# Side loads on GpSimd's queue, and the column sum of each pair's left halves by an accumulating load

## The chip, the cores and the metric

The kernel runs on one core of one Trainium2 chip. The core has TensorE (matrix products), VectorE, ScalarE (ACT here), GpSimd (POOL) and SyncE (SP), which run side by side and wait for one another by semaphores; 16 DMA engines move data between HBM and SBUF. A DMA is issued by an instruction on the queue of SP, ACT or GpSimd. The metric is the device time of one execution in microseconds. A profiled execution also leaves a trace, from which the rows below are.

## The reference, cut to what matters

One layer of a decoder trunk on 256 tokens of width 2048, all in float32: an input norm; one projection `w_in` to three mixers and their gates; the mixers (a gated short convolution, a causal spatial gating, a 31-tap convolution branch), each projected by `w_branch`, gated and summed; an output projection and a norm; a feed-forward net and a norm.

```
x = layer_norm(x, ln_in_g, ln_in_b)
z = x @ w_in                                   # 2048 -> 13312
merged = sum over n of sigmoid(g_n + gate_bias_n) * (y_n @ w_branch[n])
mix = merged @ w_out                           # 2048 -> 2048
x = layer_norm(2**0.25 * x + mix, ln_mix_g, ln_mix_b)
h_gate, h_up = split(x @ w_ffn_in)             # 2048 -> 2 x 5632
ffn = (silu(h_gate) * h_up) @ w_ffn_out        # 5632 -> 2048
x = layer_norm(2**0.25 * x + ffn, ln_ffn_g, ln_ffn_b)
```

The kernel reads some 300 MB of weights once, and multiplies each by the 256 tokens, held as two blocks of 128.

## The kernel before, in words

**Split products.** TensorE works in float32r. A float32 operand is split in two float32r parts: `hi` is the cast (ACT, L128), `lo` is what the cast left off (VectorE, L130). A product is three matrix products: hi·hi, hi·lo, lo·hi (L205 to L207 in `gemm`, L251 to L253 in `product`). Every weight tile goes through this split, which is by far the largest work of ACT and VectorE.

**The plan.** `plan` is one list of 552 weight tiles of 512 KB, in the order of use. A tile of a plain chunk is two blocks of 128 rows by 512 columns; a tile of a block product (`add_block`) is 128 rows by 1024 columns, a left and a right half. `pump(i)` is called before each step of a product: it loads up to 5 tiles ahead (`load_one`, L184, on SP's queue, four buffers `wraw`), splits up to 3 ahead (`split_one`; seven buffers each of `whi` and `wlo`), and runs up to two pieces of background work. The program order of loads and splits follows from that; in time they run as far ahead as the buffers let them.

**Pairs.** In a block product, some pairs of weight rows are done by a scheme of seven products instead of eight (Strassen's, in Winograd's form): 57 pairs, two or three to a block. A pair takes two tiles, `t0` and `t1`, whose halves are called b12, b11 (left and right of `t0`) and b22, b21 (of `t1`). `split_pair` (L133 to L161) makes on VectorE the sums t1 = b11+b12, t3 = b12+b22 (in place, over b12), t2 = t1+b22 and t4 = t2+b21, in the tile `tsum` and in `wraw`, four additions of 128 x 512 (L140), and splits four tiles: `second` (`t1`), `low` (t1 and t2), `first` (`t0`, now t3 and b11) and `last` (t4). `gemm_block` then takes them in the order second, low, first, last: products with b21, b22, t1, t2, b11, t3, t4. A step of a single tile is 12 matrix products of 512 columns, a pair 21. After a block's last pair one ACT copy (L295) and four VectorE additions (L296 to L299) combine the shared sums; the block's four results are evacuated after its last step (`evac`, with `total`, L656). A block of the branches, of `ac`, `ah`, `ab` and of `o` has six singles, a pair, three singles, a pair, three singles; the feed-forward blocks have three pairs (gate blocks `fg` and up blocks `fu`, numbered by the first of their two column groups f) or two (`fo`). A switch ADDER, off, would have made two of the additions by accumulating DMAs from SBUF.

**The order around the change.** `clock` counts steps (a pair is two). `defer(fn, after)` puts work off by so many steps; `run_deferred` runs what is due after each step. Each engine takes its instructions in the program's order, so an instruction that waits holds up what stands behind it on its engine. Scratch rows of 128 x 512 come from a pool of 8, `tmp`.

**The output projection `o`.** The block ("o", 0) makes column groups 0 and 1 (clock 0 to 16), two plain chunks of 8 steps groups 2 and 3. Their results are added to the normed input, scaled: `residual(j)` (L811 to L819) broadcasts 512 entries of `ln_in_g` and `ln_in_b` to all partitions (two DMAs on ACT's queue, L804), loads the two token blocks of x into `R` (SP, L815), and does two VectorE operations on each (L816, L818). It was due at clock 7, 9, 11 and 13 for j = 0 to 3. `R` lies in a pool opened (`open_ffn`) in place of those of the branches, so its first writer waits for their last readers, the transposes of `merged`. `evac_o` (L823, L825) adds the projection and takes norm statistics.

**Feed-forward.** Eleven column groups in three parts. `mix_residual(j)` (two broadcasts by L804, then L849 and L850 on `R`) is run in the up blocks f = 0 and f = 2. The last norm's eight rows are loaded by the same `bcast` (L804) before the last two chunks. Norm statistics end with two small GpSimd operations (L325, L328).

Of the kernel before, what the change touches and what calls it, by code (L numbers as in the profile page):

```python
# [41 lines left out]
SUMS_AT = 5  # L42
X_PAIRS = 2
LEAD = 6
ADDER = False

OFF_AB, OFF_AC, OFF_AH = 0, DA, 2 * DA
OFF_BU, OFF_BV = 3 * DA, 4 * DA
# [5 lines left out]
def trunk_kernel(ctx: ExitStack, tc: tile.TileContext, x, ln_in_g, ln_in_b, w_in, gate_bias,  # L54
# [23 lines left out]
    def cols(j, w=NW):  # L78
        return slice(j * w, (j + 1) * w)
# [53 lines left out]
    def split_pair(t0, t1):  # L133


        b12, b11, b22, b21 = t0[:, 0, :], t0[:, 1, :], t1[:, 0, :], t1[:, 1, :]
        ts = wp.tile([P, 3, NW], F32, name="tsum", bufs=1)

        def add(out, a, b):
            nc.vector.tensor_tensor(out=out, in0=a, in1=b, op=ALU.add)  # L140

        add(ts[:, 0, :], b11, b12)
        if ADDER:
            nc.gpsimd.dma_start(out=b12, in_=b22, accum_op=ALU.add)
        else:
            add(b12, b12, b22)
        add(ts[:, 1, :], ts[:, 0, :], b22)
        second = split_tile(t1)
        if ADDER:
            nc.scalar.copy(out=ts[:, 2, :], in_=ts[:, 1, :])  # L150
            nc.gpsimd.dma_start(out=ts[:, 2, :], in_=b21, accum_op=ALU.add)
        else:
            add(ts[:, 2, :], ts[:, 1, :], b21)
        low = split_tile(ts[:, 0:2, :])
        first = split_tile(t0)
        last = split_tile(ts[:, 2:3, :], 1)

        def part(pair, i):
            return pair[0][:, i, :], pair[1][:, i, :]

        return {"b11": part(first, 1), "t3": part(first, 0), "b22": part(second, 0), "b21": part(second, 1),  # L161
                "t1": part(low, 0), "t2": part(low, 1), "t4": part(last, 0)}
# [18 lines left out]
    def load_one():  # L181
        j = state["dma"]
        t = wp.tile([P, KT, NW], F32, name="wraw", bufs=RAW_BUFS)
        nc.sync.dma_start(out=t, in_=plan[j])  # L184
        raw_t[j] = t
        state["dma"] += 1

    def may_split():
# [23 lines left out]
    def defer(fn, after=DEFER, banks=True):  # L212


        deferred.append((clock[0] + after, fn, banks))
# [585 lines left out]

    def bcast(src, j):
        t_ = new_tmp()
        nc.scalar.dma_start(out=t_, in_=src[0:1, cols(j)].broadcast_to([P, NW]))  # L804
        return t_

    stm = stats_tile("stm", 4)
    lg2, lb2 = (a.rearrange("(o d) -> o d", o=1) for a in (ln_in_g, ln_in_b))
    res = {}

    def residual(j):  # L811
        gj, bj = bcast(lg2, j), bcast(lb2, j)
        for t in range(NT):
            xr = res[t, j] = R[t][:, cols(j)]
            nc.sync.dma_start(out=xr, in_=x2d[cols(t, P), cols(j)])  # L815
            nc.vector.scalar_tensor_tensor(out=xr, in0=xr, scalar=mv_in[t][:, 0:1], in1=gj,  # L816
                                           op0=ALU.subtract, op1=ALU.mult)
            nc.vector.scalar_tensor_tensor(out=xr, in0=xr, scalar=rs_in[t], in1=bj,  # L818
                                           op0=ALU.mult, op1=ALU.add)  # L819

    def evac_o(t, j, ps, add=None):
        dst = R[t][:, cols(j)]
# [13 lines left out]
            for q in range((S_PAIRS + 1) // 2):  # L836
                defer(lambda q=q: token_sums(xS, 2 * q, kept[0, q], kept[1, q], min(2, S_PAIRS - 2 * q)), 6 + q, False)

    for j in range(4):
        defer(lambda j=j: residual(j), 7 + 2 * j, False)  # L840
    gemm_block(("o", 0), mT, lambda i, t, h, ps, add: evac_o(t, h, ps, add), mTS)
    for j in (2, 3):
        gemm(("o", j), mT, lambda t, ps, j=j: evac_o(t, j, ps), skew=SKEW if j == 3 else 0)

    def mix_residual(j):
        gj, bj = bcast(ln_mix_g, j), bcast(ln_mix_b, j)
        for t in range(NT):
            cs = R[t][:, cols(j)]
            nc.vector.scalar_tensor_tensor(out=cs, in0=cs, scalar=ALPHA, in1=gj, op0=ALU.mult, op1=ALU.mult)  # L849
            nc.vector.scalar_tensor_tensor(out=cs, in0=bj, scalar=ALPHA, in1=cs, op0=ALU.mult, op1=ALU.add)  # L850


    stf = stats_tile("stf", 4)
# [99 lines left out]
```

## Time and profile before

| | us |
|---|---|
| Median of 3 runs (lowest to highest) | 1556.21 (1555.82 to 1557.3) |
| The profiled execution, device time | 1555.2 |
| Its span in the trace | 1553.5 |
| TensorE busy | 1522.1 |
| VectorE busy | 1340.1 |
| ACT busy | 771.1 |
| GpSimd busy | 16.4 |

The span is from the first to the last instruction that the profile shows; the 1.7 us around it belong to the device time. Busy times count an engine's work once, however much of it overlaps; register and semaphore instructions and the issue of DMAs are not in them. In rows, PE is TensorE's products, PEld its weight loads, DVE VectorE; a `q` after an engine's name means its sequencer, which issues DMAs. `out<-in` names the tiles, L the line. PEclk is the granted clock as a share of full speed. An engine's idle time in brackets stands before the instruction, with what ended it.

### The profile page before, as it was taken

Reading aid. Unit: us, or ns where it says so; the run is one execution under the profiler, and the core shown is the slowest. Engines: PE = TensorE matmul, PEld = TensorE weight load, DVE = VectorE, ACT = ScalarE, POOL = GpSimd, SP = SyncE. Lnnn points to the kernel's source line nnn. Section 1 sums busy time; section 2 is a strip of 40 time slices with the busy share of each in tenths; the row PEclk is TensorE's granted clock in tenths of the full one; section 3 lists DMA queues with packets and bytes.
Section 4 is the critical chain, followed back from the end, with each engine's and each line's share of the span. In section 5 each row is a group of like instructions: output and inputs, shape, how many; then the busy total and the mean of one; then the engine's idle time right before and its main releaser. Section 6 shows DMA issues by size and latency. Waiting matters only on the chain. (4 is left out here: it accounts for less than half of the span.)

```text
span 1553.5 us, 18790 instructions
## 1 busy us (share of the span) xinstructions
PE 1522.1 (98%) x6799; PEld 1247.2 (80%) x6799; DVE 1340.1 (86%) x1792; ACT 771.1 (50%) x885; POOL 16.4 (1%) x28
## 2 busy tenths in 40 slices
PE   7999999999999999999999999999999999999997
PEld 5888888888888888888877888788888878888885
DVE  7699999987789878778879799988899988889677
ACT  5544445444455454545426454555555554455451
POOL 1000000000000000000000000000000000000000
PEclk9999999999999999999999999999999999999999
DMA  6866656566665665756755666566665666666654
GB/s 215 277 191 186 182 150 227 167 220 199 201 204 161 217 201 182 251 169 228 239 181 162 218 190 215 178 229 204 191 195 171 202 193 199 205 190 203 217 176 149
DMA packets 105363, 308.13 MB, mean 198 GB/s; under 512 B 9908, under 2 KB 11028, under 8 KB 105270
## 3 DMA queue, kind: packets, MB, share of 16 engines
q1 hardware_dynamic: 99158, 295.38, 60.2%
q10 hardware_dynamic: 6112, 11.55, 2.5%
q8 instruction: 53, 0.87, 0.2%
q14 instruction: 40, 0.33, 0.1%
HBM read 304.80 MB, written 2.10 MB: 198 GB/s over the span
## 5 line engine op out<-in xcount | busy, mean ns | idle before, releaser
L128 ACT CAST whi<-wraw 128x1024 fp32r<-128x1024 f32 x551 | 577.2, 1051 | 539.3 <-PE acc L253 152.3
L130 DVE TENSOR_TENSOR wlo<-wraw,whi 128x1024 fp32r<-128x1024 f32 x551 | 666.4, 1220 | 127.7 <-ACT whi L128 124.1
L251 PE MATMUL acc<-whi,th 128*128 128x512 f32 x1235 | 485.7, 393 | 2.1 <-ACT th L316 1.0
L252 PE MATMUL acc<-wlo,th 128*128 128x512 f32 x1235 | 481.6, 390 | 0.0
L253 PE MATMUL acc<-whi,tl 128*128 128x512 f32 x1235 | 481.1, 390 | 0.0
L251 PEld LDWEIGHTS acc<-whi,th 128*128 128x128 f32 x1235 | 231.9, 188 | 52.0 <-ACT th L316 1.8
L253 PEld LDWEIGHTS acc<-whi,tl 128*128 128x128 f32 x1235 | 231.7, 188 | 50.3 <-DVE tl L317 0.3
L252 PEld LDWEIGHTS acc<-wlo,th 128*128 128x128 f32 x1235 | 232.0, 188 | 47.5
L206 PE MATMUL acc<-wlo,th 128*128 128x512 f32 x496 | 194.6, 393 | 3.4 <-DVE wlo L130 3.4
L205 PE MATMUL acc<-whi,th 128*128 128x512 f32 x496 | 195.7, 395 | 0.2 <-ACT th L316 0.2
L207 PE MATMUL acc<-whi,tl 128*128 128x512 f32 x496 | 194.4, 393 | 0.0
L128 ACT CAST whi<-tsum 128x1024 fp32r<-128x1024 f32 x114 | 95.3, 836 | 145.6 <-DVE tsum L140 122.6
L130 DVE TENSOR_TENSOR wlo<-tsum,whi 128x1024 fp32r<-128x1024 f32 x114 | 108.5, 952 | 12.5 <-ACT whi L128 12.5
L206 PEld LDWEIGHTS acc<-wlo,th 128*128 128x128 f32 x496 | 93.8, 189 | 23.5 <-DVE wlo L130 4.1
L207 PEld LDWEIGHTS acc<-whi,tl 128*128 128x128 f32 x496 | 93.8, 189 | 20.2 <-DVE tl L317 0.4
L205 PEld LDWEIGHTS acc<-whi,th 128*128 128x128 f32 x496 | 93.7, 189 | 20.1 <-ACT th L316 0.8
L563 DVE SCALAR_TENSOR_TENSOR cv<-pad,cw,cv 128x256 f32<-128x256 f32 x240 | 101.4, 482 | 0.0
L140 DVE TENSOR_TENSOR tsum<-tsum,wraw 128x512 f32<-128x512 f32 x114 | 78.1, 685 | 0.6
L251 PE MATMUL acc<-whi,yh 128*128 128x512 f32 x192 | 75.7, 394 | 0.0
L252 PE MATMUL acc<-wlo,yh 128*128 128x512 f32 x192 | 75.5, 393 | 0.0
L253 PE MATMUL acc<-whi,yl 128*128 128x512 f32 x192 | 74.7, 389 | 0.0
L140 DVE TENSOR_TENSOR tsum<-wraw 128x512 f32<-128x512 f32 x57 | 39.2, 688 | 29.9 <-DMA wraw<-in_w_in_dram 21.1
(157 smaller groups left out, 1172.0 us busy)
## 6 DMA issues: line engine op xcount, KB each, us to landing
wraw<-in_w_in_dram SPq DMA_DIRECT2D x208, 512.0 KB, 4.0
wraw<-in_w_ffn_in_dram SPq DMA_DIRECT2D x176, 512.0 KB, 4.3
wraw<-in_w_ffn_out_dram SPq DMA_DIRECT2D x88, 512.0 KB, 4.5
wraw<-in_w_branch_dram SPq DMA_DIRECT2D x48, 512.0 KB, 5.0
wraw<-in_w_out_dram SPq DMA_DIRECT2D x32, 512.0 KB, 6.2
gb<-in_gate_bias_dram ACTq DMA_DIRECT2D x12, 256.0 KB, 3.4
R<-in_x_dram SPq DMA_DIRECT2D x8, 256.0 KB, 4.6
x<-in_x_dram SPq DMA_DIRECT2D x2, 512.0 KB
```

The costliest lines, as they stand in the source:

```text
L128: nc.scalar.copy(out=hi, in_=t)
L130: nc.vector.tensor_tensor(out=lo, in0=t, in1=hi.bitcast(F32), op=ALU.subtract)
L140: nc.vector.tensor_tensor(out=out, in0=a, in1=b, op=ALU.add)
L205: nc.tensor.matmul(ps, lhsT=xh[:, k, ts], rhs=hi[:, kk, :], start=first, stop=False)
L206: nc.tensor.matmul(ps, lhsT=xh[:, k, ts], rhs=lo[:, kk, :], start=False, stop=False)
L207: nc.tensor.matmul(ps, lhsT=xl[:, k, ts], rhs=hi[:, kk, :], start=False, stop=last)
L251: nc.tensor.matmul(ps, lhsT=ah, rhs=bh, start=first, stop=False)
L252: nc.tensor.matmul(ps, lhsT=ah, rhs=bl, start=False, stop=False)
L253: nc.tensor.matmul(ps, lhsT=al, rhs=bh, start=False, stop=last)
L563: nc.vector.scalar_tensor_tensor(out=cv[:, b, :], in0=pad[:, b, q:q + S], scalar=w_, in1=cv[:, b, :], op0=ALU.mult, op1=ALU.add)
```

## The change

`load_one` issues, right behind the load of a pair's first tile, a second DMA on GpSimd's queue, which reads the left half of the second tile (b22) from HBM and adds it to the left half of the first (b12) where that lies in SBUF. So t3 = b12+b22 needs no VectorE addition. `split_pair` splits the second tile first, and then makes three additions, from it: t2 = b11 + t3, t1 = t2 - b22, t4 = t2 + b21; `first` is split before `low`. The switch ADDER goes.

The row broadcasts of `bcast` are issued on GpSimd's queue instead of ACT's. The eight x loads of the residual are issued together on GpSimd's queue at clock 3 (`residual_rows`) instead of on SP's. `residual(j)` issues its broadcasts at clock 5, 7, 15 and 17 and its VectorE operations four steps later, at 9, 11, 19 and 21; `mix_residual` keeps its place, with its VectorE operations three steps after its broadcasts.

```diff
--- before.py
+++ after.py
@@ -42,7 +42,6 @@
 SUMS_AT = 5
 X_PAIRS = 2
 LEAD = 6
-ADDER = False
 
 OFF_AB, OFF_AC, OFF_AH = 0, DA, 2 * DA
 OFF_BU, OFF_BV = 3 * DA, 4 * DA
@@ -136,23 +135,15 @@
         b12, b11, b22, b21 = t0[:, 0, :], t0[:, 1, :], t1[:, 0, :], t1[:, 1, :]
         ts = wp.tile([P, 3, NW], F32, name="tsum", bufs=1)
 
-        def add(out, a, b):
-            nc.vector.tensor_tensor(out=out, in0=a, in1=b, op=ALU.add)
-
-        add(ts[:, 0, :], b11, b12)
-        if ADDER:
-            nc.gpsimd.dma_start(out=b12, in_=b22, accum_op=ALU.add)
-        else:
-            add(b12, b12, b22)
-        add(ts[:, 1, :], ts[:, 0, :], b22)
+        def add(out, a, b, op=ALU.add):
+            nc.vector.tensor_tensor(out=out, in0=a, in1=b, op=op)
+
         second = split_tile(t1)
-        if ADDER:
-            nc.scalar.copy(out=ts[:, 2, :], in_=ts[:, 1, :])
-            nc.gpsimd.dma_start(out=ts[:, 2, :], in_=b21, accum_op=ALU.add)
-        else:
-            add(ts[:, 2, :], ts[:, 1, :], b21)
+        add(ts[:, 1, :], b11, b12)
+        add(ts[:, 0, :], ts[:, 1, :], b22, ALU.subtract)
+        add(ts[:, 2, :], ts[:, 1, :], b21)
+        first = split_tile(t0)
         low = split_tile(ts[:, 0:2, :])
-        first = split_tile(t0)
         last = split_tile(ts[:, 2:3, :], 1)
 
         def part(pair, i):
@@ -183,6 +174,8 @@
         t = wp.tile([P, KT, NW], F32, name="wraw", bufs=RAW_BUFS)
         nc.sync.dma_start(out=t, in_=plan[j])
         raw_t[j] = t
+        if j in fast:
+            nc.gpsimd.dma_start(out=t[:, 0, :], in_=plan[j + 1][:, 0, :], accum_op=ALU.add)
         state["dma"] += 1
 
     def may_split():
@@ -801,22 +794,27 @@
 
     def bcast(src, j):
         t_ = new_tmp()
-        nc.scalar.dma_start(out=t_, in_=src[0:1, cols(j)].broadcast_to([P, NW]))
+        nc.gpsimd.dma_start(out=t_, in_=src[0:1, cols(j)].broadcast_to([P, NW]))
         return t_
 
     stm = stats_tile("stm", 4)
     lg2, lb2 = (a.rearrange("(o d) -> o d", o=1) for a in (ln_in_g, ln_in_b))
-    res = {}
-
-    def residual(j):
+    def residual_rows():
+        for j in range(4):
+            for t in range(NT):
+                nc.gpsimd.dma_start(out=R[t][:, cols(j)], in_=x2d[cols(t, P), cols(j)])
+
+    def residual(j, wait):
         gj, bj = bcast(lg2, j), bcast(lb2, j)
-        for t in range(NT):
-            xr = res[t, j] = R[t][:, cols(j)]
-            nc.sync.dma_start(out=xr, in_=x2d[cols(t, P), cols(j)])
-            nc.vector.scalar_tensor_tensor(out=xr, in0=xr, scalar=mv_in[t][:, 0:1], in1=gj,
-                                           op0=ALU.subtract, op1=ALU.mult)
-            nc.vector.scalar_tensor_tensor(out=xr, in0=xr, scalar=rs_in[t], in1=bj,
-                                           op0=ALU.mult, op1=ALU.add)
+
+        def go():
+            for t in range(NT):
+                xr = R[t][:, cols(j)]
+                nc.vector.scalar_tensor_tensor(out=xr, in0=xr, scalar=mv_in[t][:, 0:1], in1=gj,
+                                               op0=ALU.subtract, op1=ALU.mult)
+                nc.vector.scalar_tensor_tensor(out=xr, in0=xr, scalar=rs_in[t], in1=bj,
+                                               op0=ALU.mult, op1=ALU.add)
+        defer(go, wait, False)
 
     def evac_o(t, j, ps, add=None):
         dst = R[t][:, cols(j)]
@@ -836,18 +834,22 @@
             for q in range((S_PAIRS + 1) // 2):
                 defer(lambda q=q: token_sums(xS, 2 * q, kept[0, q], kept[1, q], min(2, S_PAIRS - 2 * q)), 6 + q, False)
 
-    for j in range(4):
-        defer(lambda j=j: residual(j), 7 + 2 * j, False)
+    defer(residual_rows, 3, False)
+    for j, at in enumerate((5, 7, 15, 17)):
+        defer(lambda j=j: residual(j, 4), at, False)
     gemm_block(("o", 0), mT, lambda i, t, h, ps, add: evac_o(t, h, ps, add), mTS)
     for j in (2, 3):
         gemm(("o", j), mT, lambda t, ps, j=j: evac_o(t, j, ps), skew=SKEW if j == 3 else 0)
 
     def mix_residual(j):
         gj, bj = bcast(ln_mix_g, j), bcast(ln_mix_b, j)
-        for t in range(NT):
-            cs = R[t][:, cols(j)]
-            nc.vector.scalar_tensor_tensor(out=cs, in0=cs, scalar=ALPHA, in1=gj, op0=ALU.mult, op1=ALU.mult)
-            nc.vector.scalar_tensor_tensor(out=cs, in0=bj, scalar=ALPHA, in1=cs, op0=ALU.mult, op1=ALU.add)
+
+        def go():
+            for t in range(NT):
+                cs = R[t][:, cols(j)]
+                nc.vector.scalar_tensor_tensor(out=cs, in0=cs, scalar=ALPHA, in1=gj, op0=ALU.mult, op1=ALU.mult)
+                nc.vector.scalar_tensor_tensor(out=cs, in0=bj, scalar=ALPHA, in1=cs, op0=ALU.mult, op1=ALU.add)
+        defer(go, 3, False)
 
 
     stf = stats_tile("stf", 4)
```

## Rows read from the trace of the kernel before

**Rows 1.** The page's first part: busy us, share of the span, instructions

```profile
PE 1522.1 (98%) x6799; PEld 1247.2 (80%) x6799; DVE 1340.1 (86%) x1792; ACT 771.1 (50%) x885; POOL 16.4 (1%) x28
```

**Rows 2.** Stretches: us, busy PE, PEld, DVE, ACT, POOL; PEclk; DMA share; GB/s

```profile
0.00:40.00 40.00, 29.42 (x127) 20.41 (x128) 31.67 (x52) 23.18 (x41) 5.93 (x12) 0.91 0.68 217
...
760.00:800.00 40.00, 36.55 (x154) 29.73 (x153) 31.83 (x40) 14.31 (x15) 0.00 (x0) 0.96 0.53 175
...
960.00:1000.00 40.00, 38.71 (x167) 30.89 (x167) 37.63 (x47) 17.95 (x21) 0.00 (x0) 1.00 0.63 189
...
1080.00:1120.00 40.00, 40.00 (x177) 32.87 (x176) 37.31 (x45) 20.26 (x22) 0.00 (x0) 1.00 0.64 195
...
1240.00:1280.00 40.00, 37.56 (x169) 29.49 (x168) 35.78 (x45) 19.76 (x23) 0.00 (x0) 1.00 0.63 191
...
1520.00:1560.00 40.00, 22.43 (x99) 18.22 (x98) 23.63 (x33) 3.16 (x3) 3.41 (x4) 0.90 0.33 120
```

**Rows 3.** TensorE's waits: for whom, us in total, times, longest

```profile
PE acc L310 <- DVE tmp L432: 9.3, 6, 3.4
PE acc L206 <- DVE wlo L130: 3.4, 1, 3.4
...
PE acc L252 <- DVE wlo L130: 1.2, 2, 0.8
```

**Rows 4.** A group of instructions on VectorE: busy us, mean ns, idle before, releasers

```profile
L140 DVE TENSOR_TENSOR wraw<-wraw 128x512 f32<-128x512 f32 x57 | 39.2, 687 | 17.7 <-DMA wraw<-in_w_in_dram 11.7 <-DMA wraw<-in_w_ffn_out_dram 3.5 <-DMA wraw<-in_w_ffn_in_dram 2.0
```

**Rows 5.** Timeline of VectorE, 774 to 787: start us, us, instruction

```profile
776.59 1.42 DVE L816 SCALAR_TENSOR_TENSOR R<-R,mvin,tmp 128x512 f32<-128x512 f32 x2 [1.80 <-DMA tmp<-in_ln_in_g_dram]
779.46 1.41 DVE L818 SCALAR_TENSOR_TENSOR R<-R,rsin,tmp 128x512 f32<-128x512 f32 x2 [1.46 <-DMA tmp<-in_ln_in_b_dram]
...
786.77 1.22 DVE L130 TENSOR_TENSOR wlo<-wraw,whi 128x1024 fp32r<-128x1024 f32 x1
```

**Rows 6.** Stretches of 10 us around the `o` block's evacuation

```profile
790.00:800.00 10.00, 10.00 (x39) 8.07 (x39) 6.00 (x6) 4.34 (x5) 0.00 (x0) 0.86 0.77 255
800.00:810.00 10.00, 10.00 (x46) 8.27 (x45) 6.95 (x8) 3.03 (x3) 0.00 (x0) 1.00 0.80 269
```

**Rows 7.** L184 from 978 to 979.5, and VectorE's timeline from 986

```profile
L184 SPq DMA_DIRECT2D wraw<-in_w_ffn_in_dram x1: 327/327/327, 978.7 to 978.7; - x1
...
DMA to landing us min/median/max: 4.4/4.4/4.4
...
988.06 1.22 DVE L130 TENSOR_TENSOR wlo<-wraw,whi 128x1024 fp32r<-128x1024 f32 x1
```

**Rows 8.** Timelines of VectorE and TensorE, third pairs of f=4 and f=6

```profile
1106.21 1.23 DVE L130 TENSOR_TENSOR wlo<-tsum,whi 128x1024 fp32r<-128x1024 f32 x1 [0.66 <-ACT whi L128]
...
1113.81 0.39 PE L251 MATMUL acc<-whi,xS 128*128 128x512 f32 x1
...
1245.74 1.23 DVE L130 TENSOR_TENSOR wlo<-tsum,whi 128x1024 fp32r<-128x1024 f32 x1 [0.47 <-ACT whi L128]
...
1248.87 0.39 PE L251 MATMUL acc<-whi,xS 128*128 128x512 f32 x1
```

**Rows 9.** DMA issues: engine, count, KB each, median us to landing

```profile
gb<-in_gate_bias_dram ACTq DMA_DIRECT2D x12, 256.0 KB, 3.4
R<-in_x_dram SPq DMA_DIRECT2D x8, 256.0 KB, 4.6
...
tmp<-in_ln_in_b_dram ACTq DMA_DIRECT2D x4, 256.0 KB, 6.7
```

**Rows 10.** SP's timeline, L815 and L175 (ns min/median/max), TensorE's timeline

```profile
742.09 1.28 SPq L815 DMA_DIRECT2D R<-in_x_dram  x3
...
L815 SPq DMA_DIRECT2D R<-in_x_dram x8: 328/430/589, 742.1 to 752.6; - x8
...
L175 POOL TENSOR_TENSOR wlo<-wraw,whi x1: 2545/2545/2545, 9.5 to 9.5; 128x1024 fp32r<-128x1024 f32 x1
...
761.77 0.39 PE L251 MATMUL acc<-whi,sum 128*128 128x512 f32 x1
```

## The prediction

> **What bounds the kernel now.** I read the busy shares first, then the table by stretches, then who TensorE waited for, and only then the two or three places where it waited. TensorE is busy 1522.1 us of a span of 1553.5 [rows 1], so all that any edit can win back is 31.4 us. The stretches say where these lie [rows 2]: 10.6 us in the first 40 us (the input norm), 33.5 - 22.4 = 11.1 us at the end (last norm and stores). The change touches neither. The middle has 31.4 - 10.6 - 11.1 = 9.7 us: 3.45 in 760 to 800, 2.44 in 1240 to 1280, 1.29 in 960 to 1000, and small change elsewhere. VectorE is the busiest of the others, 1340.1 us, and in a feed-forward stretch such as 1080 to 1120 it works 37.3 of 40 us while TensorE never stops: it is nearly a second bound, but not the bound. By waits, the start is 9.3 us on L432; the largest in the middle is one wait of 3.4 us of L206 on VectorE's lo half (L130) [rows 3].
>
> So VectorE work removed is worth something only near those gaps, and VectorE stalls added cost something only where TensorE's reserve of split weights is short. A usual reserve: in the gate block f=4 the pair's `low` halves start on VectorE at 1106.21 (done 1107.4) and their first product starts on TensorE at 1113.81: over 6 us [rows 8]. In the up block f=6 the third pair's start at 1245.74 (done 1247.0) and are used at 1248.87: 1.9 us.
>
> **The change, part by part.**
>
> *One addition per pair leaves VectorE.* L140 `wraw<-wraw` is 39.2 us in 57 pieces of 687 ns [rows 4]; three of this kind stay. 39.2 us come off VectorE, nearly all of it beside busy TensorE. It pays in two places. In the up block f=2 (960 to 1000) TensorE waited 1.2 us for lo halves [rows 3]; by the block's third pair three additions, 2.06 us, are gone ahead of it, so I count all 1.2. In 1240 to 1280 (end of the up block f=6) 2.44 us are idle [rows 2], behind VectorE's evacuation and then behind transposes; VectorE reaches them up to 2.06 us earlier, but part is a chain of latencies, so I take half, 1.2 (bounds 0 and 2.4).
>
> *The new order in a pair.* The split of the second tile comes first, `first` ahead of `low`. In VectorE work from the pair's start, second is ready after 1.22 instead of 3.3 us, `low` after 1.22 + 3 x 0.69 + 2 x 1.22 = 5.7 instead of 5.2, the last after 6.4 instead of 7.1. TensorE takes second, low, first, last, so only `low` loses, 0.5 us, under a reserve of 6: nothing. With the reserve gone it is 0.5 us a pair, 28 us; in the two tight blocks the additions saved in earlier pairs cover it.
>
> *57 accumulating loads.* Each waits on GpSimd's queue for the first tile's own load, then adds 256 KB from HBM. Traffic grows by 57 x 0.262 = 14.9 MB, 5% of the 308 MB; the DMA engines are busy some 60 to 65% of such stretches [rows 2], so the plain loads slow little: 0.5 us, bounds 0 and 2. What matters is X, the time from the first tile's landing to the sum's. The trace shows no accumulating transfer and none from GpSimd. Plain transfers of this size land in a median 3.4 to 6.7 us after issue, the x rows in 4.6 [rows 9]. An accumulation has to read what it adds to as well: bounds 3.4 and 2 x 4.6 = 9.2 us; I take 5, nearest the x rows and a little over.
>
> When is it needed? Take the tightest pair, the third of the up block f=2. Its first tile is issued at 978.7 and lands 4.4 us later, at 983.1; the split of the second tile starts on VectorE at 988.06 [rows 7]. In the new order one addition ahead of it is gone, so it starts near 987.4 and is done near 988.6: there the first addition wants the sum, 5.5 us after the landing. X = 5 costs nothing. A late sum stops VectorE in order, with splits and evacuations behind it, and no other work can pass. Where loads are just in time, the second tile still has to land, be cast (1.05 us) and split (1.22 us), and the reserve is 5 us or more: hidden too.
>
> The Trainium skill, "DMA: Bandwidth & Descriptors", section on the GpSimd path, fits 2.0 us plus bytes over 436 GB/s to one such plain DMA. For 256 KB that estimate is 2.6 us, under every row here; by it X would leave 2.9 us of margin, and the sum would be the same.
>
> *Residual and side loads.* This is the larger part. Before, the residual of column group 3 is issued at the end of the `o` block: VectorE waits 1.80 us for ln_in_g and 1.46 us for ln_in_b, does 1.42 + 1.41 us of residual between, and only then evacuates the block; the next lo half starts at 786.77, is done at 788.0, and TensorE waits 3.4 us for it, so wanted it at 784.6 [rows 3, 5]. After that the granted clock is 0.86 for 10 us, a mix of the 1.2 and 2.4 GHz levels, and 39 matmuls begin where 46 do at full clock: 7 x 0.22 = 1.5 us more [rows 6]. The change sends both residuals of groups 2 and 3 behind the evacuation (steps 19 and 21) with loads four steps ahead. Ahead of the evacuation VectorE then has 3.3 us of waiting and 2.8 us of work less, besides group 2's 2.8 us, so that lo half is done at least 6.1 us earlier, near 781.9, before TensorE wants it: 3.4 + 1.5 = 4.9 us gained. What is late next is nothing I can find: the moved 2 x 2.8 us of VectorE work fall into 790 to 810, where it has 7 us idle [rows 6].
>
> The cost stands on GpSimd's queue. In program order eight x loads, two row broadcasts and then the second `o` pair's accumulating load are issued. The x loads wait until R's place is free, which SP's rows put at 742.09 [rows 10]. One issue takes 0.33 to 0.59 us on SP; a GpSimd issue is not in the trace, and its only whole-tile operation took 2.5 us [rows 10]: bounds 0.33 and 2.5, and I take 1.0, towards the issues. Ten issues: 752.1; landed 757.1; then three additions and two splits, 4.5 us: `low` at 761.6, wanted at 761.77 [rows 10]. Just in time, so 0.5 us for it (0 at the low end, 15 at the high one). GpSimd's norm operations come after stages without pairs, and find the queue empty. The 24 row broadcasts leave ACT, which is half idle [rows 1]: nothing. The x loads leave SP, whose weight loads stand four buffers ahead: nothing. [...]
>
> **Sum.** 4.9 + 1.2 + 1.2 = 7.3 gained, 0.5 + 0.5 + 0.5 = 1.5 lost: 5.8 us. The profiled execution took 1555.2 us (span 1553.5 and 1.7 around it): 1549.4. The median of the runs is 1.0 us above it, so 1550.4. With every gap of the middle closed it would be 9.7 + 1.5 = 11.2 us, 1545.
>
> **Rivals.**
>
> *The sum lands late (slower).* Place: the second and third pair of the up block f=2, all three of f=6, where the reserve is short [rows 3, 8]. It decides at X = 5.5. At X = 9.2 VectorE stands 3.7 us in each: 5 x 3.7 = 18.5 us, less the 5.8: 1569. If it also eats the 2.7 us that VectorE has left in other stretches [rows 2], 1580; at X = 7, 1558. For it: nothing here shows an accumulation, and loads meet others in flight. Against: where VectorE is behind, the tiles lie longer before it asks. The Trainium skill, "Collectives: The Full Stack", section on the bandwidth ceiling, says a reduction in the DMA path needs two source reads and ran at half the rate of a copy; that would make this rival likelier, and no run here shows it yet.
>
> *The gain goes to GpSimd's queue (no change).* At 1.5 us an issue the second `o` pair's sum is issued at 757.1, `low` is ready at 766.6 and TensorE waits 4.8 us: 5.8 + 0.5 - 4.8 = 1.5 us left, 1554.7. For it: ten issues in a row, none of them priced. Against: VectorE has group 0's and 1's residual work behind that pair now instead of ahead.
>
> *It doesn't do what it says.* The additions are hidden anyway and the moved residuals stop VectorE at steps 19 and 21 as they did at 13: only the small gains stay, 2.4 - 1.5: 1555.3.
>
> **Chances.** Forecast 0.58 (own range 1545 to 1553), late sum 0.22, queue 0.13, no effect 0.07. A measurement of this kernel can tell about 0.2%, 3.1 us, from no change: faster 0.58, same 0.20, slower 0.22. The range reaches from all gaps closed, 1545, into the late sum at X near 8.5, 1566.
>
> **What would show it.** Right: no wait of L206 near 785 and full clock after it; VectorE's busy time down by about 39 us; the additions of a pair never waiting on the accumulating load for long. Wrong: `tsum` waiting on a DMA in most pairs with TensorE's waits on lo halves grown (late sum); a TensorE gap near 760 (queue); the gap near 785 moved to 800 (no effect). A rise of TensorE's idle time in the middle above 9.7 us refutes the forecast.

## The result, and the profile after

The changed kernel takes 1641.29 us (median of 4 runs, 1639.25 to 1644.7) against 1556.76 us for the kernel before on the same chip: ratio 1.0541, 95% interval 1.0526 to 1.0556. It is 84.5 us slower. The forecast was 1550.4 with a range up to 1566.0, so the prediction was wrong in sign and the time lies outside its range. The execution profiled here took 1644.7 us, with a span of 1643.0.

The busy shares of the changed kernel (busy us, share of the span, instructions; before: [rows 1]):

```profile
PE 1551.9 (94%) x6799; PEld 1258.1 (77%) x6799; DVE 1303.7 (79%) x1735; ACT 772.8 (47%) x885; POOL 83.4 (5%) x117
```

GpSimd's 83.4 us hold the issue of its DMAs, which the profile counts as work on that engine. VectorE has 36.4 us less work, much as forecast. But the span grew by 1643.0 - 1553.5 = 89.5 us, so VectorE now idles 339.3 us instead of 213.4, and TensorE 91.1 instead of 31.4. TensorE's 6799 matmuls also take 29.8 us more; it runs in parts at a lower granted clock (mean 0.98, before 0.995).

The same stretches as in [rows 2], and two more (columns as there):

```profile
0.00:40.00 40.00, 30.44 (x130) 21.09 (x131) 31.12 (x53) 24.07 (x43) 5.74 (x12) 0.91 0.68 221
200.00:240.00 40.00, 33.80 (x151) 27.40 (x150) 31.52 (x57) 14.74 (x17) 1.71 (x2) 0.91 0.48 133
...
760.00:800.00 40.00, 36.13 (x156) 29.21 (x156) 27.20 (x39) 13.10 (x17) 8.74 (x15) 0.91 0.67 210
960.00:1000.00 40.00, 36.92 (x165) 29.16 (x166) 35.40 (x48) 20.80 (x26) 2.54 (x3) 1.00 0.63 175
1080.00:1120.00 40.00, 40.00 (x178) 33.10 (x177) 32.71 (x38) 18.39 (x20) 0.86 (x1) 1.00 0.62 200
1320.00:1360.00 40.00, 35.87 (x146) 28.09 (x145) 29.83 (x36) 17.97 (x21) 1.71 (x2) 0.89 0.63 193
```

The start is unchanged (30.44 against 29.42). The loss is spread over the middle, where the pairs are made: in 21 of the 35 stretches of 40 us from 200 to 1600, TensorE stands for more than 1 us, mostly for 2 to 6. In nine of them the granted clock is a mix of its two levels (0.89 to 0.96); in others, as 960 to 1000, it stays at 1.00, and 1080 to 1120 has pairs and no hole at all. Stretches shift against those of before by up to 88 us, so this is a picture of what such stretches look like now and no comparison row by row.

TensorE's waits (for whom, us in total, times, longest; before: [rows 3]), from the changed kernel:

```profile
PE acc L245 <- DVE wlo L129: 29.1, 17, 4.6
PE acc L303 <- DVE tmp L425: 8.3, 6, 3.1
PE acc L303 <- DVE a L866: 7.6, 6, 2.9
```

L245 and L129 are L252 and L130 of before. Where TensorE waited 1.2 us in total for those lo halves, it now waits 29.1, about half of the 59.7 us that its idle time grew; most of the rest are waits for other results, such as the `a` of the third line, 0.8 us before.

And VectorE's own groups (busy us, mean ns, idle time just before them and its releasers), one of before that stands beside [rows 4], then those of the changed kernel:

```profile
L140 DVE TENSOR_TENSOR tsum<-wraw 128x512 f32<-128x512 f32 x57 | 39.2, 688 | 29.9 <-DMA wraw<-in_w_in_dram 21.1 <-DMA wraw<-in_w_ffn_out_dram 6.8 <-DMA wraw<-in_w_ffn_in_dram 1.3
```

```profile
L139 DVE TENSOR_TENSOR tsum<-tsum,wraw 128x512 f32<-128x512 f32 x114 | 75.1, 686 | 4.3 <-DMA wraw<-in_w_in_dram 2.4 <-DMA wraw<-in_w_ffn_in_dram 1.3
...
L139 DVE TENSOR_TENSOR tsum<-wraw 128x512 f32<-128x512 f32 x57 | 39.3, 690 | 170.7 <-DMA wraw<-in_w_in_dram 71.4 <-issue 44.3 <-DMA wraw<-in_w_ffn_out_dram 29.8
```

The additions wait 170.7 + 4.3 = 175.0 us, where before they waited 29.9 + 17.7 + 0.6 = 48.2 (0.6 is that of the two additions that write and read `tsum`): 126.8 more. Less the 36.4 us of work that left VectorE, that is 90.4 us, beside the 89.5 that the span grew. The sums agree, but agreement is not yet a cause; the experiments are for that. The 44.3 us put down to "issue" are waits for the sum too: each of the 39 additions that waited begins 0.08 us behind the landing of its own accumulating load.

**One pair, read closely.** The second pair of `w_in`'s `ac` group. VectorE from 357 us of the changed kernel:

```profile
358.55 1.82 DVE L129 TENSOR_TENSOR wlo<-tsum,whi 128x1024 fp32r<-128x1024 f32 x2
368.29 0.69 DVE L139 TENSOR_TENSOR tsum<-wraw 128x512 f32<-128x512 f32 x1 [7.92 <-DMA wraw<-in_w_in_dram]
368.90 2.35 DVE L129 TENSOR_TENSOR wlo<-wraw,whi 128x1024 fp32r<-128x1024 f32 x2
```

ScalarE's hi halves and GpSimd's accumulating load in that time:

```profile
358.49 1.99 ACT L127 CAST whi<-wraw 128x1024 fp32r<-128x1024 f32 x2
361.11 1.05 ACT L127 CAST whi<-wraw 128x1024 fp32r<-128x1024 f32 x1 [0.63 <-DMA wraw<-in_w_in_dram]
```

```profile
363.88 0.87 POOL L178 DMA_DIRECT2D wraw<-in_w_in_dram  x1 [16.82 <-DMA wraw<-in_w_in_dram]
```

And TensorE, whose next product needs a lo half of an earlier tile:

```profile
365.14 0.39 PE L244 MATMUL acc<-whi,th 128*128 128x512 f32 x1
370.17 0.80 PE L245 MATMUL acc<-wlo,th 128*128 128x512 f32 x1 [4.64 <-DVE wlo L129]
```

The lo half of this pair's own second tile comes long after its first addition (VectorE from 370 us):

```profile
376.03 2.35 DVE L129 TENSOR_TENSOR wlo<-wraw,whi 128x1024 fp32r<-128x1024 f32 x2
```

VectorE is done at 360.37 and stands until 368.29, for the sum. Three hi halves are ready by 362.16, so three lo halves could be made, 3 x 1.22 us; but they stand behind the addition on VectorE's queue. GpSimd's load was issued at 363.88, when the first tile had landed; the sum let the addition start 4.4 us later. (Over all pairs, 20.5 of the 170.7 us pass before the load is issued, so for the first tile, and 150.2 behind it.) TensorE ran dry at 365.5 and stood 4.64 us. SyncE's weight loads stand too, since lo halves free their buffers (waits of its queue, 357 to 372):

```profile
SPq L175 <- DVE wlo L129: 12.5, 3, 11.1
SPq L175 <- DVE tsum L139: 2.0, 1, 2.0
```

So a late sum delays the next loads as well. The stretches around it show the second price, the clock (columns as in [rows 2]): 37 matmuls begin in the 10 us behind the hole at a granted 0.83, where 46 do at full clock.

```profile
360.00:370.00 10.00, 5.53 (x25) 4.25 (x23) 2.08 (x3) 1.53 (x2) 0.87 (x1) 1.00 0.38 98
370.00:380.00 10.00, 9.83 (x37) 8.01 (x38) 7.57 (x9) 5.32 (x6) 0.00 (x0) 0.83 0.61 188
380.00:390.00 10.00, 10.00 (x46) 8.29 (x45) 7.78 (x8) 5.30 (x7) 0.00 (x0) 1.00 0.85 288
```

Over all 57 pairs of this trace, the first addition starts ahead of its own pair's second lo half in 38; those 38 carry 163.5 of the 170.7 us. From the first tile's landing to the sum's it takes a median of 5.7 us. In 39 pairs the first landing is not recorded, and 4.6 us after its issue is taken; in the 18 others the median is 5.2 us.

### The profile page after: what moved, and what is told of

Same layout as the page of the kernel before. It is cut to its first block, busy times and chain, and to the rows that moved or that the text cites. A ratio compares the mean times of both kernels' runs of the same rounds, so it can differ in the third digit from the quotient of the medians.

```text
span 1643.0 us, 19015 instructions
## 1 busy us (share of the span) xinstructions
PE 1551.9 (94%) x6799; PEld 1258.1 (77%) x6799; DVE 1303.7 (79%) x1735; ACT 772.8 (47%) x885; POOL 83.4 (5%) x117
## 5 line engine op out<-in xcount | busy, mean ns | idle before, releaser
L129 DVE TENSOR_TENSOR wlo<-wraw,whi 128x1024 fp32r<-128x1024 f32 x551 | 663.0, 1221 | 120.0 <-ACT whi L127 116.4
L245 PE MATMUL acc<-wlo,th 128*128 128x512 f32 x1235 | 491.1, 398 | 22.6 <-DVE wlo L129 22.6
L244 PE MATMUL acc<-whi,th 128*128 128x512 f32 x1235 | 494.0, 400 | 14.0 <-ACT tok L565 5.9
L245 PEld LDWEIGHTS acc<-wlo,th 128*128 128x128 f32 x1235 | 236.5, 192 | 75.5 <-DVE wlo L129 27.6
L244 PEld LDWEIGHTS acc<-whi,th 128*128 128x128 f32 x1235 | 236.4, 191 | 68.9 <-ACT tok L565 6.3
L246 PEld LDWEIGHTS acc<-whi,tl 128*128 128x128 f32 x1235 | 236.2, 191 | 55.0 <-DVE tl L310 3.7
L199 PE MATMUL acc<-wlo,th 128*128 128x512 f32 x496 | 194.2, 393 | 2.9 <-DVE wlo L129 2.8
L198 PE MATMUL acc<-whi,th 128*128 128x512 f32 x496 | 195.4, 395 | 0.8 <-ACT whi L127 0.7
L139 DVE TENSOR_TENSOR tsum<-wraw 128x512 f32<-128x512 f32 x57 | 39.3, 690 | 170.7 <-DMA wraw<-in_w_in_dram 71.4
L127 ACT CAST whi<-tsum 128x1024 fp32r<-128x1024 f32 x114 | 91.6, 834 | 140.4 <-DVE tsum L139 123.4
L199 PEld LDWEIGHTS acc<-wlo,th 128*128 128x128 f32 x496 | 93.4, 188 | 23.4 <-DVE wlo L129 4.6
L129 DVE TENSOR_TENSOR wlo<-tsum,whi 128x1024 fp32r<-128x1024 f32 x114 | 104.3, 953 | 7.5 <-ACT whi L127 7.3
L198 PEld LDWEIGHTS acc<-whi,th 128*128 128x128 f32 x496 | 93.5, 189 | 21.0 <-ACT whi L127 1.5
L200 PEld LDWEIGHTS acc<-whi,tl 128*128 128x128 f32 x496 | 93.4, 188 | 20.4 <-DVE tl L310 0.8
L245 PE MATMUL acc<-wlo,yh 128*128 128x512 f32 x192 | 75.5, 393 | 0.0
```

The lines of the kernel that those rows point to most:

```text
L127: nc.scalar.copy(out=hi, in_=t)
L129: nc.vector.tensor_tensor(out=lo, in0=t, in1=hi.bitcast(F32), op=ALU.subtract)
L139: nc.vector.tensor_tensor(out=out, in0=a, in1=b, op=op)
L198: nc.tensor.matmul(ps, lhsT=xh[:, k, ts], rhs=hi[:, kk, :], start=first, stop=False)
L199: nc.tensor.matmul(ps, lhsT=xh[:, k, ts], rhs=lo[:, kk, :], start=False, stop=False)
L200: nc.tensor.matmul(ps, lhsT=xl[:, k, ts], rhs=hi[:, kk, :], start=False, stop=last)
```

## The experiments

Theory A: the sum comes some 5.7 us after the first tile, and the addition that needs it stands on VectorE's queue ahead of lo halves that are ready; that wait is the price. Rival B: 14.9 MB more traffic slow the weight loads. Rival C: the side loads and their queue cost. Times of the kernel before in the runs compared: 1557.05 for the first four, 1557.6 to 1557.7 for the others.

**Side loads alone** (`side_only`). The diff's second part on the kernel before: `bcast` and the x rows on GpSimd's queue, the residual of groups 2 and 3 moved behind the evacuation; pairs as before.

```
-        nc.scalar.dma_start(out=t_, in_=src[0:1, cols(j)].broadcast_to([P, NW]))
+        nc.gpsimd.dma_start(out=t_, in_=src[0:1, cols(j)].broadcast_to([P, NW]))
...
+    defer(residual_rows, 3, False)
+    for j, at in enumerate((5, 7, 15, 17)):
+        defer(lambda j=j: residual(j, 4), at, False)
```

> The side loads and the moved residual alone; pairs with four VectorE additions and no accumulating load. Theories A and B: 1549 to 1556 us, the 3.4 us wait of TensorE near 785 gone. Theory C: over 1600.

1552.9 us, ratio 0.997 [0.9958, 0.9981]: 4.2 us faster. Rival C falls. The stretch that held the stall at 785 before is nearly whole, 39.93 us busy instead of 36.55 [rows 2], though 800 to 810 has lost some (7.97 where [rows 6] has 10.00):

```profile
760.00:800.00 40.00, 39.93 (x176) 32.71 (x176) 37.11 (x47) 15.25 (x15) 2.19 (x4) 1.00 0.68 211
790.00:800.00 10.00, 9.93 (x44) 7.90 (x43) 9.93 (x11) 3.16 (x3) 0.00 (x0) 1.00 0.60 195
800.00:810.00 10.00, 7.97 (x28) 5.54 (x27) 5.98 (x7) 3.15 (x3) 0.00 (x0) 0.86 0.78 255
```

**Accumulating loads alone** (`acc_only`). The diff's first part (`split_pair` and the load in `load_one`) on the kernel before.

```
+        if j in fast:
+            nc.gpsimd.dma_start(out=t[:, 0, :], in_=plan[j + 1][:, 0, :], accum_op=ALU.add)
```

> The accumulating loads and the new pair order alone; residual and side loads as before the change. Theory A (the sum lands 5.7 us after the first tile, and the first addition of a pair stands on VectorE's queue ahead of lo halves that are ready, so VectorE stands still): 1635 to 1650 us, VectorE's waits of the pair additions on DMA again near 170 us. Theory B (the 57 extra transfers slow the weight loads): the same time, 1635 to 1650. Theory C (the side loads on GpSimd's queue are the loss): 1550 to 1565.

1653.64 us, ratio 1.0618 [1.06, 1.0636]. All of the loss, and 12 us more than the whole change has, lies in this part. That the side loads are worth 12 us beside it and 4.2 us alone was not followed up.

**The additions held back** (`pinned`). The whole change, but the three additions of a pair may be placed on VectorE's queue only behind the second tile's lo half, the order that the prediction had taken for given. `last_lo[0]` is the lo half that the program wrote last, here that of the second tile.

```
+        with tc.issue_after(last_lo[0].ins):
             add(ts[:, 1, :], b11, b12)
             add(ts[:, 0, :], ts[:, 1, :], b22, ALU.subtract)
             add(ts[:, 2, :], ts[:, 1, :], b21)
```

> The whole change, with one edge more in the order: the three additions of a pair stand behind the lo half of the pair's second tile on VectorE's queue. Same transfers, same work. Theory A: the wait of the additions falls below 60 us in total and the time to 1550 to 1580 us. Theory B: 1630 to 1645, nothing gained, since the traffic is the same.

1575.69 us, ratio 1.0119 [1.0098, 1.014]. The place on the queue, with the small shifts of other instructions that it brings along, is worth 1641.3 - 1575.7 = 65.6 us, with the same loads landing no earlier (a median of 6.2 us behind the first tile). Waits of VectorE in this kernel, for the sum 20.7 us over all pairs instead of 170.7:

```profile
DVE wlo L129 <- ACT whi L127: 201.5, 190, 4.8
DVE tsum L141 <- DMA wraw<-in_w_ffn_in_dram: 6.8, 5, 2.3
DVE tsum L141 <- DMA wraw<-in_w_in_dram: 6.5, 5, 1.8
```

**The traffic without the wait** (`traffic`). The kernel before plus 57 accumulating loads of 384 columns, three quarters of the bytes, into a row that nobody reads.

```
+        if j in fast:
+            nc.gpsimd.tensor_copy(out=side[:, 0:1], in_=t[:, 0, 0:1])
+            nc.gpsimd.dma_start(out=side, in_=plan[j + 1][:, 0, 0:384], accum_op=ALU.add)
...
+    nc.gpsimd.memset(side, 0.0)
```

> The kernel before, with 57 accumulating loads on GpSimd's queue into a scratch row that nothing reads (384 of the 512 columns, for want of room), each behind a small GpSimd copy that waits for the pair's first tile. Theory A: 1556 to 1564 us, since nothing waits for the loads. Theory B: most of the 84 us, over 1610.

1567.24 us, ratio 1.0063 [1.0049, 1.0077]: 10 us, above theory A's figure and far below rival B's. Part of it is what the memset at the start costs, which the last run below takes out.

**VectorE's fourth sum in the changed kernel** (`order_noacc`). The whole change without the accumulating load.

```
         second = split_tile(t1)
+        add(b12, b12, b22)
...
-        if j in fast:
-            nc.gpsimd.dma_start(out=t[:, 0, :], in_=plan[j + 1][:, 0, :], accum_op=ALU.add)
```

> The whole change, but with the pair's fourth sum made by VectorE from the two landed tiles again instead of by the accumulating load (the new order inside a pair and the moved side loads stay). Theory A (the late sum and its early place on VectorE's queue cost the time): nothing is left but the gain of the side loads, 1549 to 1555 us, VectorE's additions wait on loads no longer than before (about 48 us in all) and TensorE's gaps in the middle are below 10 us. Rival E (the new order inside a pair costs by itself, because the low halves of the second and third sum come 0.5 us later in each of 57 pairs): 1560 to 1580 us with TensorE waiting on lo halves in many pairs.

1550.26 us, ratio 0.9952 [0.9937, 0.9966]. It beats both kernels: 7.3 us under the kernel before, 91 under the changed one. Its three `tsum` additions, too, begin ahead of the second lo half in 26 of 57 pairs, and the fourth sum does in 40; it waits 41.2 us in all, for the second tile:

```profile
L139 DVE TENSOR_TENSOR tsum<-wraw 128x512 f32<-128x512 f32 x57 | 39.3, 689 | 1.2
L139 DVE TENSOR_TENSOR wraw<-wraw 128x512 f32<-128x512 f32 x57 | 39.2, 688 | 41.2 <-DMA wraw<-in_w_in_dram 14.5 <-DMA wraw<-in_w_ffn_out_dram 13.0 <-DMA wraw<-in_w_ffn_in_dram 11.1
```

So an early place is harmless by itself where what the addition waits for comes soon. It takes both, the place and the late sum.

**The order inside a pair alone** (`order_only`). The same `split_pair` on the kernel before, side loads as before.

```
         second = split_tile(t1)
+        add(b12, b12, b22)
         add(ts[:, 1, :], b11, b12)
...
         first = split_tile(t0)
         low = split_tile(ts[:, 0:2, :])
```

> The kernel before with the new order inside a pair alone (second tile's split first, its own fourth sum still made by VectorE, side loads as before). The kernel with this order and the new side loads ran at 1550.3, the one with the new side loads alone at 1552.9. If the order inside a pair gains by itself: 1553 to 1556 us, 1 to 4 us under the kernel before. If it is neutral and the difference between those two was scatter: 1556 to 1558.5 us.

1557.0 us, ratio 0.999 [0.9978, 1.0002]: neutral. The interval of `order_noacc` overlaps that of the side loads alone, so no gain of the order is shown.

**The pin without the loads** (`noacc_pinned`), and **with unread loads** (`noacc_pinned_traffic`). `order_noacc` with all four additions held behind the second lo half; then the 57 unread loads on top.

```
+        with tc.issue_after(last_lo[0].ins):
+            add(b12, b12, b22)
             add(ts[:, 1, :], b11, b12)
```

> The kernel with VectorE's own fourth sum and all additions of a pair held behind the second tile's lo half, as in the pinned kernel but with no accumulating load. It asks what of the pinned kernel's remaining 19 us over the kernel before (1575.7 against 1557.0) is the hand-set order itself. D1/D2 (the order is free; late sums and traffic make the rest): 1550 to 1556 us. D3 (taking the scheduler's freedom away costs): 1562 to 1575 us, with VectorE idle behind ScalarE's hi halves while additions could have run.

> The previous kernel plus 57 accumulating loads of 384 columns into a scratch row that nobody reads, each behind its pair's first tile: traffic and queue without anyone waiting for the sum. Measured on top of the kernel before, such loads cost 10 us. D1 (the sums still late in 15 pairs, 20.7 us of VectorE waiting, make about half of the rest): the same 8 to 12 us over the kernel without them, 1560 to 1566 us, and 10 to 14 us stay for the waits. D2 (it is all traffic): 1568 to 1575 us, within 5 us of the pinned kernel.

1560.31 us (ratio 1.0014 [1.0003, 1.0025]) and 1574.68 us (1.0107 [1.0087, 1.0126]). Holding the additions back costs 10 us by itself: VectorE now waits 171.8 us for ScalarE's hi halves where it waited 133.5, with additions that it might have done. The two lines, of `order_noacc` and of `noacc_pinned`:

```profile
DVE wlo L129 <- ACT whi L127: 133.5, 131, 5.6
```

```profile
DVE wlo L129 <- ACT whi L127: 171.8, 146, 5.3
```

The unread loads add 14.4 us. With these two, `pinned` is reached to 1 us. But the memset at the start, which `pinned` has not, is in the 14.4 (3 to 4 us by the last run below), and `pinned` has the full bytes and one addition less; so there the waits for the sum cost little: 1 us by these numbers, some 5 with the fill taken out. The pin by itself lies between what D3 and the others said, nearer D3; the rest goes as D2 said, mostly to the traffic, and the 10 to 14 us that D1 gave to the waits are not there.

**The same load, not accumulating** (`plain_pool`).

```
-            nc.gpsimd.dma_start(out=t[:, 0, :], in_=plan[j + 1][:, 0, :], accum_op=ALU.add)
+            nc.gpsimd.dma_start(out=t[:, 0, :], in_=plan[j + 1][:, 0, :])
```

> The whole change, but the load on GpSimd's queue replaces the left half instead of adding to it, so the pair's fourth sum is left out of the computation; everything else, its issue point, its bytes and who waits for it, is the same. If the accumulation itself (reading what it adds to) makes the sum late: from issue to landing well under the 4.7 to 5.7 us of the accumulating loads, about 3 to 4 us, and 1595 to 1620 us. If the place in the queue behind the weight loads and GpSimd's way of issuing make it late: 4.5 to 5.5 us from issue to landing, additions waiting 150 to 175 us, and 1630 to 1645 us.

1587.72 us, ratio 1.0188 [1.0171, 1.0205], faster than either theory said: 54 us go with the accumulation, though the order on VectorE's queue is the same instruction by instruction and the bytes are too. The time from the first tile's landing to this load's falls only from 5.7 to 4.8 us (from the load's own issue, from 4.9 to 4.2), and the first additions' waits from 170.7 to 126.5 us, by 44.2. 0.7 to 0.9 us in each of 57 pairs is 40 to 51 us, so nearly all that the sum comes earlier is gained. What the other 10 us of the 54 are, later loads, the clock or the lighter traffic, was not separated. The loads of the changed kernel and of this one (engine, count, KB, median us to landing):

```profile
wraw<-in_w_ffn_in_dram POOLq DMA_DIRECT2D x27, 256.0 KB, 4.9
wraw<-in_w_in_dram POOLq DMA_DIRECT2D x18, 256.0 KB, 4.7
...
wraw<-in_w_ffn_out_dram POOLq DMA_DIRECT2D x10, 256.0 KB, 5.7
```

```profile
wraw<-in_w_ffn_in_dram POOLq DMA_DIRECT2D x27, 256.0 KB, 4.3
wraw<-in_w_in_dram POOLq DMA_DIRECT2D x18, 256.0 KB, 3.8
...
wraw<-in_w_ffn_out_dram POOLq DMA_DIRECT2D x10, 256.0 KB, 4.7
```

**Unread loads in the kernel with the early order** (`noacc_traffic`, `noacc_traffic_plain`, `noacc_traffic2`). The 57 loads of `traffic` on `order_noacc`: accumulating, then replacing, then accumulating with the row filled at the first pair rather than at the start (the cut is the step to this last one).

```
-            nc.gpsimd.tensor_copy(out=side[:, 0:1], in_=t[:, 0, 0:1])
+            w_ = 1 if side_ready else 384
+            side_ready.append(1)
+            nc.gpsimd.tensor_copy(out=side[:, 0:w_], in_=t[:, 0, 0:w_])
...
-    nc.gpsimd.memset(side, 0.0)
+    side_ready = []
```

> The kernel with VectorE's fourth sum (1550.3 us) plus 57 accumulating loads of 384 columns into a scratch row that nobody reads, each issued on GpSimd's queue behind a small copy that waits for the pair's first tile. Such loads cost 10 us on the kernel before and 14 us on the kernel with pinned additions. Theory T1 (accumulating packets keep the DMA engines busy and delay the weight tiles) and T2 (any load on this queue costs it, by its issue or its share of the engines) both say 1559 to 1566 us here; if the earlier cost hung on those two orders, 1551 to 1556 us.

> The same with loads that replace instead of adding: same bytes, issue points and order of every engine. T1 (the accumulation is what costs): 1551 to 1555 us, the queue's share of the DMA engines down from about 6.4% to 4%. T2 (any load there costs): 1559 to 1566 us, within 2 us of the accumulating ones.

1558.52 us (ratio 1.0002 [0.9992, 1.0013]) and 1555.09 us (0.9988 [0.9977, 0.9999]). Neither theory had it whole, and the first 45 us suggest why: with the row's fill on GpSimd, the start is slower by 16 matmuls. Stretches of `order_noacc`, `noacc_traffic` and `noacc_traffic2`:

```profile
0.00:45.00 45.00, 35.66 (x158) 25.35 (x159) 34.31 (x62) 27.82 (x48) 5.90 (x12) 0.92 0.68 217
```

```profile
0.00:45.00 45.00, 32.40 (x142) 23.05 (x143) 33.19 (x60) 25.61 (x45) 7.40 (x13) 0.89 0.64 209
```

```profile
0.00:45.00 45.00, 35.45 (x153) 24.79 (x154) 35.20 (x61) 27.93 (x48) 6.08 (x12) 0.92 0.67 215
```

> The kernel with VectorE's fourth sum (1550.3 us) and 57 accumulating loads of 384 columns into an unread scratch row, as before, but the scratch row is first filled at the first pair (about 200 us) instead of by GpSimd at the start. In the earlier version (1558.5) TensorE began 142 matmuls in the first 45 us where the kernel without the loads began 158: 16 x 0.227 = 3.6 us, before any of the loads. If that fill was the cause of the slow start and the loads cost the rest: 1554 to 1556 us and 155 to 160 matmuls in the first 45 us. If the slow start is not the fill, or the loads cost all 8 us: 1557.5 to 1560 us.

1554.86 us (0.9988 [0.9972, 1.0004]), as the first of the two expectations had it, though 153 matmuls are two short of it. So the fill did cost the slow start, and the accumulating traffic costs 1554.9 - 1550.3 = 4.6 us when nobody waits for it (each of the two medians is known to some 2 us). In the earlier two kernels, whose order of instructions is the same on every engine, the accumulating loads cost 3.4 us more than the plain ones.

**The account.** From `order_noacc` (1550.3) to the changed kernel (1641.3) it is 91 us: about 5 for the traffic (three quarters of its bytes were tried) and so some 86 for waiting for the sum, which is a difference and not measured by itself. With the larger costs of unread loads in the two other orders, less the fill, it would be 6 to 11 and 80 to 85; rival B has no more than that. Of the wait, 54 disappear when the same load doesn't accumulate, and about 66 when the additions merely stand one lo half later, in spite of what that costs by itself. How much of the 86 is the wait in the pair itself and how much the weight loads that start later behind it was not separated, nor why unread loads cost 4.6 us with one order and up to 14 with another (of which the fill at the start is 3 to 4).

## Why the prediction was wrong, step by step

- **When the sum is needed: the step that failed.** It said of the third pair of the up block f=2 that VectorE starts the second tile's split "near 987.4 and is done near 988.6: there the first addition wants the sum, 5.5 us after the landing", and concluded "X = 5 costs nothing". For that pair it holds: in the changed trace its addition starts at 1041.35, right behind the lo half of 1040.21, with no wait. It was then taken as the tightest case for all 57. But VectorE does not take its instructions in the order in which `split_pair` writes them (what the description of the kernel calls the program's order is that of the built program); there the first addition stands ahead of the second lo half in 38 of 57 pairs, and with no lo half between, it wants the sum when the first tile has barely landed. `pinned`, which makes the assumption true, gives back 65.6 of the 84.5 us. The trace of before could have warned: in 17 of its 57 pairs the second lo half runs ahead of an addition that `split_pair` writes before it, as in that very pair, 988.06 [rows 7] ahead of an addition at 989.80. The line of before (VectorE, 986 to 990.2) and the two of the changed kernel (VectorE, 1038 to 1044):

```profile
989.80 0.68 DVE L140 TENSOR_TENSOR tsum<-tsum,wraw 128x512 f32<-128x512 f32 x1
```

```profile
1040.21 1.22 DVE L129 TENSOR_TENSOR wlo<-wraw,whi 128x1024 fp32r<-128x1024 f32 x1
1041.35 0.68 DVE L139 TENSOR_TENSOR tsum<-wraw 128x512 f32<-128x512 f32 x1
```

- **"Where loads are just in time ... hidden too".** [rows 8] are of feed-forward blocks (the line at 1106.21 is of the second pair of f=4, not the third) and show nothing of the `w_in` blocks. There the trace has the reserve: before, from the end of `low`'s lo half to its first product it is 4.1 to 13.9 us in the 18 `w_in` pairs, and about 5 or more in 16 of them. But 22 of the 38 early additions wait more than 4 us, up to 7.9, and the loads start later as well; over all pairs the median of that reserve falls from 5.9 to 2.0 us.
- **X itself.** Taken 5 us, bounds 3.4 and 9.2; the median is 5.7, just over the 5.5 at which the prediction let a late sum begin to cost. By its own rule that is 0.2 us in each of five pairs: this size was not the fault. A GpSimd issue, taken 1.0 us, takes 0.54 for a plain load and 0.86 for an accumulating one. The Trainium skill, "Collectives: The Full Stack", section on the bandwidth ceiling, has a reduction in the DMA path at half a copy's rate: the trace agrees in the engines' time below, while the landing came only 0.6 to 1.0 us later in the three groups shown above. The 2.6 us that the prediction estimated for a plain load from the Trainium skill, "DMA: Bandwidth & Descriptors", section on the GpSimd path, lies under the 3.8 to 4.7 us measured here.
- **The rival "the sum lands late".** It had the sign and the sign to look for, `tsum` waiting on a DMA in most pairs. It placed the price in five pairs and got 1569 to 1580; its place was wrong, so its price was too. (1580 takes the 2.7 us of one stretch about four times over, which the prediction doesn't say.)
- **39.2 us off VectorE.** Right as work (36.4 measured), but the 2.4 us counted for the two up blocks did not come: the matmuls of 960 to 1000 now run from 1010 to 1053 with 4.2 us of idle time instead of 1.3, those of 1240 to 1280 from 1311 to 1359 with 6.3 instead of 2.4. What the saved work is worth without the late sum, no run shows.
- **Residual and side loads, 4.9 us.** Right: 4.2 by the medians of `side_only`. "What is late next is nothing I can find" was not quite: 2 us of gaps came up between 802 and 807.
- **The new order in a pair, nothing.** Right: `order_only`, 1557.0 against 1557.6.
- **Traffic, 0.5 us (0 to 2).** Mis-sized: 4.6 us with three quarters of the bytes.
- **The third 0.5 us of the losses.** No run shows this term, a cost of GpSimd's queue at the end: from the last matmul to the end of the span it is 11.1 us before and after the change, and 1.7 us lie outside the span both times.
- **GpSimd's queue at the second `o` pair, 0.5 us.** Near, 0.9 us, but by luck: two sizes were off in opposite ways. The eight x loads take 4.25 us to issue instead of 8; then that pair's load, issued at 788.4, 3.0 us behind its tile, lands among the x rows 11.4 us later, at 799.7, instead of 5. VectorE waits 3.4 us for it, TensorE 0.9 for that `low`. GpSimd from 760 us, VectorE from 794:

```profile
788.37 0.89 POOL L178 DMA_DIRECT2D wraw<-in_w_out_dram  x1 [0.19 <-issue]
```

```profile
799.77 0.69 DVE L139 TENSOR_TENSOR tsum<-wraw 128x512 f32<-128x512 f32 x1 [3.42 <-DMA wraw<-in_w_out_dram]
```

## What to carry to other kernels

Before work moves from an engine to a transfer, read in the trace what really stands behind the instruction that will wait for it: an engine takes its queue in the built order, which need not be the order of the source, and one late operand holds everything ready behind it. Work taken off an engine that isn't the bound need not show in the time, while a wait put on it costs what exceeds the reserve in front of the bound, and can cost again through later loads and the clock. If an experiment needs a helper (here a row to be filled), look at the first stretch for what the helper itself costs.

## What the runs showed of the hardware

Accumulation doubled the time that such a load took of the DMA engines here. GpSimd's queue in the changed kernel and in `plain_pool` (packets, MB, share of 16 engines' span):

```profile
q0 software_dynamic: 10768, 23.34, 7.7%
```

```profile
q0 software_dynamic: 7120, 23.34, 4.7%
```

In `order_noacc` the side loads alone are 2560 packets and 1.8% of 1549.9, 27.9 us:

```profile
q0 software_dynamic: 2560, 8.39, 1.8%
```

That leaves 8208 packets and 98.6 us for the 57 accumulating loads, 4560 and 46.6 us for plain ones of the same bytes: 144 packets instead of 80 each, and 2.1 times the time. GpSimd is also longer at issuing them, min, median, max in ns, for the changed kernel and `plain_pool`:

```profile
L178 POOL DMA_DIRECT2D wraw<-in_w_ffn_in_dram x27: 845/851/909, 913.2 to 1495.6; - x27
```

```profile
L178 POOL DMA_DIRECT2D wraw<-in_w_ffn_in_dram x27: 536/538/538, 882.5 to 1438.6; - x27
```

And the x rows, which landed in a median of 4.6 us from SyncE's queue [rows 9] (5.5 in `traffic`, 6.8 in `order_only`), take 7.1 to 8.8 us from GpSimd's in the kernels with that part of the change, eight issued in a row.
